# A two-layer encoder trunk on one core: order of the weight loads, arithmetic on GpSimd, and the output projections

## The chip, the cores and the metric

The kernel runs on one core of a Trainium2 chip. A core has TensorE (PE, matrix products; its weight loads are shown as PEld), VectorE (DVE), ScalarE (ACT), GpSimd (POOL) and SyncE (SP), which issues most of the transfers from HBM. The metric is the time of one execution in device microseconds, the median of three runs.

## What is computed

One sequence of 256 tokens with 1024 features passes two layers. Each layer is a token mixer and a mixture of experts (MoE), and each of the four sub-layers is normalized and scaled, shifted and gated by vectors that come from a conditioning vector c (adaLN). In short:

```python
for i in range(2):
    mod = silu(c) @ ada_w[i] + ada_b[i]                 # 6 x 1024
    sh1, sc1, g1, sh2, sc2, g2 = split(mod, 6)
    h = rms_norm(x, norm_mix_g[i]) * (1 + sc1) + sh1
    y = mla_mixer(h) if i == 0 else hyena_mixer(h)      # both end in a product with a 1024 x 1024 matrix
    x = x + g1 * y
    h = rms_norm(x, norm_ffn_g[i]) * (1 + sc2) + sh2
    x = x + g2 * hier_moe(h)                            # best of 4 groups, best 2 of its 4 experts
```

The attention (MLA) has 8 heads with low-rank q and kv. Hyena gates two long convolutions, done by Fourier transforms, whose filters come from a small network. Each of the 16 experts is a SwiGLU of 1024 to 256 to 1024. All is in 32-bit floats, so the large products run as sums of parts: a value is split into Hi (rounded) and Lo (the rest).

## The kernel before

The program runs the sub-layers one after another: attention (up to 183 us), router and MoE of layer 0 (to 361 us), Hyena (to 522 us), router and MoE of layer 1. Beside them two kinds of background work are spread into PE's gaps: the adaLN products for later sub-layers and the Hyena filters (`filt_unit`, eight units, three of them beside attention). Each engine runs its own list of instructions in order; a scheduler sets these lists when the program is built, by its own model of times, except where the code fixes the order.

Weights come through `Stream`, a ring of ten slots of 1 MB ("wt", 128 x 2048). A fixed list `order` says which block comes next; SP issues the next load as soon as a slot is free, one after the other. `st.done` gives a slot back, `st.temp` takes one for a temporary, `st.hold` keeps some free for temporaries. `moe_order` lists, for each pair of experts, four gate/up blocks (gu) and then the two down blocks (dn). The kernel computes gate and up of a pair in one step (`gate_up`) and its down product one step later (`down`). The list of attention is: five adas blocks, the four blocks of wo, the other nineteen adas blocks, and then the experts of layer 0.

An adas block is 1/8 of one of the adaLN products. `wide` (from L356) works it off as the string `WIDE` says: "p" is four matmuls of PE with the block (L389); "s" scales the block on ACT; "d" multiplies and adds on DVE (L370); "a" scales on ACT (L372) and adds on POOL (L373). "s", "d" and "a" gather several blocks into one, which then takes one product on PE. `PLAN` says how many blocks are handed out at each head of attention.

Other arithmetic on POOL before: two additions (L591) and a subtraction (L613) in each filter unit; in `split`, three of four Lo pieces of a wo block (L673; the Hi pieces are on ACT, L671); in `finish`, which adds the gated projection to x, the first half of each 128 tokens (L654; the second half on DVE, L656); in the router (`moe`), the quarters of xL, the low part of the normalized x that the experts' gather uses (L1198 and L1199, the last quarter on DVE, L1251); in `down` of layer 1, yL (L1422; in layer 0 on DVE).

Attention: `attend` takes the softmax (pr, L918 on ACT and L922 on DVE), transposes pr on PE (pT, L926), multiplies with v (oT, L931) and copies oT from PSUM on DVE (L932). The output projection comes behind the heads: for each of four wo blocks the parts oH (ACT) and oL (DVE, L956) of two heads are made, and 24 matmuls add to the four accumulators y_ps (L964). Hyena's projection has the same form, with accumulators psu (first tokens) and pse (second) and the line L1136.

The router goes from x to lg (logits), through short DVE operations L1215 to L1233 to sel (the chosen experts), to ct and rk on PE (L1239 to L1243), to the one-hot matrix OH on DVE (L1159), and to the gather xt_ps on PE (L1299, products of OH with xH and with xL), which the first gu_ps (L1388) follows. The lines L1210 start the accumulators acc with x.

## Time and profile before

| quantity | value |
|---|---|
| runs | 675.14, 676.16, 677.0 us |
| median | 676.16 us |
| profiled execution | 676.02 us |
| its span from first to last instruction | 674.2 us |
| mean granted clock of PE | 0.965 of full |

A profile belongs to one execution. The page gives, for each engine, how long it was busy. The table of stretches gives that for parts of the span, with the clock that PE was granted there (1.00 is full speed, 0.5 half). The list of waits says what ended PE's idle time: the engine, tile and line on the right of the arrow had to finish first. The views of single lines give what one instruction took.

### The profile page before, as it was taken

To read this page: it belongs to the slowest core of one execution; us is meant where nothing else is said; L and a number is where in the kernel's file an instruction comes from. 1 tells how busy PE (TensorE), PEld (TensorE's weight loads), DVE (VectorE), ACT (ScalarE), POOL (GpSimd) and SP (SyncE) were. 2 spreads that over 40 slices of the span, in tenths; PEclk is the share of its full clock that TensorE was granted. 3 is DMA by queue.
4 is the path that set the end of the run, shared out by engine and by line. 5 is a ranking of instruction groups with operands and counts; after the bars stand their busy time and mean duration, and the time that the engine had idled before them with its cause. 6 is when DMAs were issued, how large, how long until landed. Compare 5 with 4: busy or idle time off the path is not lost. (4 is left out here: it accounts for less than half of the span.)

```text
span 674.2 us, 8473 instructions
## 1 busy us (share of the span) xinstructions
PE 610.8 (91%) x3073; PEld 354.6 (53%) x3073; DVE 382.1 (57%) x826; ACT 234.8 (35%) x461; POOL 100.3 (15%) x130
## 2 busy tenths in 40 slices
PE   2998978979869899999996999999998799999996
PEld 0544435666646445445442888757776444344442
DVE  4527598898585354444567467578783832222222
ACT  2523556466243212212145554424613421111112
POOL 0001013348540000001000000000000400203023
PEclk9997998889988999989997999999999799999999
DMA  8997795664823879797987455694059368999801
GB/s 323 421 388 298 279 400 193 250 225 182 329 108 132 331 294 395 301 385 313 385 332 268 155 199 210 265 383 179 1 236 369 143 219 355 421 380 398 350 1 62
DMA packets 26819, 183.02 MB, mean 271 GB/s; under 512 B 3089, under 2 KB 3474, under 8 KB 5522
## 3 DMA queue, kind: packets, MB, share of 16 engines
q1 hardware_dynamic: 25920, 180.31, 68.2%
q10 hardware_dynamic: 850, 2.10, 0.9%
q8 instruction: 26, 0.43, 0.3%
q14 instruction: 23, 0.19, 0.1%
HBM read 181.35 MB, written 1.05 MB: 271 GB/s over the span
## 5 line engine op out<-in xcount | busy, mean ns | idle before, releaser
L1388 PE MATMUL gu_ps<-wt,XT 128*64 128x512 f32 x464 | 116.2, 604 | 7.3 <-DVEq L1452 4.2
L1388 PEld LDWEIGHTS gu_ps<-wt,XT 128*64 128x64 f32 x464 | 35.9, 138 | 69.9 <-issue 60.1
L1418 DVE TENSOR_TENSOR yg<-dn_ps,g1row 128x512 f32<-128x512 f32 x32 | 22.1, 691 | 83.5 <-PE dn_ps L1415 82.7
L1420 ACT CAST yH<-yg 128x512 fp32r<-128x512 f32 x32 | 19.8, 618 | 111.5 <-DVE yg L1418 110.4
L1415 PE MATMUL dn_ps<-wt,aT 128*64 128x512 f32 x208 | 53.6, 597 | 0.0
L1040 PE MATMUL psu<-hT,wt 128*128 128x256 f32 x192 | 44.9, 380 | 0.0
L1040 PEld LDWEIGHTS psu<-hT,wt 128*128 128x128 f32 x192 | 35.7, 190 | 9.3 <-issue 4.3
L1040 PE MATMUL psu<-zH,wt 128*128 128x256 f32 x192 | 37.9, 291 | 0.0
L1308 DVE TENSOR_SCALAR XT<-xt_ps,modA,modT 128x256 f32<-128x256 f32 x32 | 17.4, 542 | 35.5 <-ACT XT L1306 35.3
L1422 POOL TENSOR_TENSOR yL<-yg,yH 128x512 fp32r<-128x512 f32 x16 | 20.5, 1280 | 111.3 <-ACT yH L1420 110.8
L671 ACT CAST wt<-wt 128x512 fp32r<-128x512 f32 x56 | 30.8, 616 | 11.5 <-PE psu L1136 5.7
L673 DVE TENSOR_TENSOR wt<-wt 128x512 fp32r<-128x512 f32 x44 | 29.5, 709 | 6.8 <-POOL wt L673 2.4
L389 PE MATMUL ada_ps<-wt,csil 128*32 128x512 f32 x224 | 32.7, 616 | 0.1
L1306 ACT ACTIVATE XT<-xt_ps,modT,modA 128x256 f32<-128x256 f32 x32 | 17.9, 563 | 42.6 <-PE xt_ps L1299 42.5
L1040 PEld LDWEIGHTS psu<-zH,wt 128*128 128x128 f32 x192 | 30.1, 189 | 3.3 <-ACT up L1045 0.8
L1415 PEld LDWEIGHTS dn_ps<-wt,aT 128*64 128x64 f32 x208 | 16.3, 136 | 27.2 <-issue 25.9
L1299 PE MATMUL xt_ps<-OH,xH 128*128 128x256 f32 x128 | 28.7, 305 | 0.0
L1040 PE MATMUL psu<-zL,wt 128*128 128x256 f32 x96 | 27.7, 288 | 0.0
L1299 PEld LDWEIGHTS xt_ps<-OH,xH 128*128 128x128 f32 x128 | 21.2, 197 | 10.9 <-issue 4.2
L1299 PE MATMUL xt_ps<-OH,xL 128*128 128x256 f32 x128 | 26.4, 288 | 0.0
L1045 ACT ACTIVATE up<-psu,vec 128x256 f32<-128x256 f32 x24 | 11.4, 476 | 37.1 <-PE psu L1040 30.5
L1043 POOL MEMSET up<- 128x1 f32 x24 | 2.4, 100 | 141.9 <-DVE uc L1049 110.0
(367 smaller groups left out, 1227.0 us busy)
## 6 DMA issues: line engine op xcount, KB each, us to landing
wt<-in_gu SPq DMA_DIRECT2D x58, 1024.0 KB, 7.0
wt<-in_adas SPq DMA_DIRECT2D x40, 1024.0 KB, 5.7
wt<-in_dn SPq DMA_DIRECT2D x26, 1024.0 KB, 8.5
wt<-in_win SPq DMA_DIRECT2D x12, 1024.0 KB, 6.6
wt<-in_ada SPq DMA_DIRECT2D x8, 1024.0 KB, 17.3
wx<-in_dn SPq DMA_DIRECT2D x6, 1024.0 KB, 6.6
wx<-in_gu SPq DMA_DIRECT2D x6, 1024.0 KB, 8.0
wt<-in_wo SPq DMA_DIRECT2D x4, 1024.0 KB, 7.0
```

The source lines that it names most:

```text
L389: nc.tensor.matmul(q[g * 32:(g + 1) * 32, :], w.to_broadcast([P, 32]), W[:, g * 512:(g + 1) * 512], start=first, stop=(k == 7))
L671: nc.scalar.copy(Hi[:, sl], W[:, sl])
L673: eng.tensor_tensor(out=Lo[:, sl], in0=W[:, sl], in1=Hi[:, sl].bitcast(F32), op=ALU.subtract)
L1040: nc.tensor.matmul(q[:, :S], w[:, k, mm * P:(mm + 1) * P], h[:, k, :], start=(k == 0 and w is terms[0][0] and h is terms[0][1]), stop=(k = ...
L1299: nc.tensor.matmul(q[:, kk * 256:(kk + 1) * 256], src[:, t, k * P:(k + 1) * P], OH[:, t, :], start=(i == 0), stop=(i == 3))
L1306: eva = nc.scalar.activation(XT[:, k % 4, :], qv, AF.Identity, scale=a[:, k:k + 1], bias=b[:, k:k + 1])
L1308: evac[0] = nc.vector.tensor_scalar(XT[:, k % 4, :], qv, a[:, k:k + 1], b[:, k:k + 1], op0=ALU.mult, op1=ALU.add)
L1388: nc.tensor.matmul(q[i * 64:(i + 1) * 64, :], XT[h][:, k % 4, c0:c0 + CAP], GU[i][:, k % 4, :], start=(k == 0), stop=(k == 7))
L1415: nc.tensor.matmul(q[i * 64:(i + 1) * 64, :], aT[:, j, i * 64:(i + 1) * 64], DN[i][:, j, n * 512:(n + 1) * 512], start=(j == 0), stop=(j = ...
L1418: nc.vector.tensor_tensor(yg, q, grow[1][:, n * 512:(n + 1) * 512], op=ALU.mult)
L1420: nc.scalar.copy(yH, yg)
L1422: (nc.gpsimd if l else nc.vector).tensor_tensor(out=yL, in0=yg, in1=yH.bitcast(F32), op=ALU.subtract)
```

## The change

It has seven pieces.

1. Loads: wo comes behind all 24 adas blocks, and the dn blocks of a pair come behind the gu blocks of the next pair.
2. `WIDE`: mode "a" is gone. The second and third of its strings, which attention works off, are now "psddpppp" and "ppppsddd". With one product for each gathered sum, PE has 19 products in attention where it had 14; DVE has five blocks ("d") instead of seven, POOL none instead of three.
3. `filt_unit`, `finish`, `split`, the router's xL and yL of layer 1: what POOL did is done by DVE. In the router all four quarters of xL are one operation each, put behind the one-hot.
4. oH and oL are made at the end of each head, straight from PSUM, in two slots of the ring (`st.hold = 2` keeps them free); the copy of oT is gone.
5. A common `out_proj` for both projections: the first two blocks as before; then both last blocks for the first 128 tokens, and after that for the second. The slots of the last two blocks' parts come free at its end.
6. wo's first two blocks are split as before, beside the last heads.
7. In MoE of layer 0, the four slots for Hyena's first splits are held back from step 7 on instead of step 6.

```diff
-WIDE = ("pppppppp", "psdadadp", "ppsdaddd", "pppppppp", "pppppppp")
+WIDE = ("pppppppp", "psddpppp", "ppppsddd", "pppppppp", "pppppppp")
...
             for h in range(2):
                 for e in (2 * pr, 2 * pr + 1):
                     push("gu", l, e, h)
-            for e in (2 * pr, 2 * pr + 1):
-                push("dn", l, e)
+
+            for e in (2 * pr - 2, 2 * pr - 1):
+                if pr:
+                    push("dn", l, e)
+        for e in (14, 15):
+            push("dn", l, e)
...
-    for i, job in enumerate(seq):
-        if i == WO_AFTER:
-            push("wo")
+    for job in seq:
         push("adas", *job)
+    push("wo")
...
-            nc.gpsimd.tensor_tensor(out=a[:, 0, :], in0=a[:, 0, :], in1=a[:, 1, :], op=ALU.add)
+            nc.vector.tensor_tensor(a[:, 0, :], a[:, 0, :], a[:, 1, :], op=ALU.add)
...
-        nc.gpsimd.tensor_tensor(out=hh[1], in0=hh[0], in1=hh[1], op=ALU.subtract)
+        nc.vector.tensor_tensor(hh[1], hh[0], hh[1], op=ALU.subtract)
...
-                if n == 0:
-                    nc.gpsimd.tensor_tensor(out=x[:, t, sl], in0=x[:, t, sl], in1=tmp, op=ALU.add)
-                else:
-                    nc.vector.tensor_tensor(x[:, t, sl], x[:, t, sl], tmp, op=ALU.add)
+                nc.vector.tensor_tensor(x[:, t, sl], x[:, t, sl], tmp, op=ALU.add)
...
-            eng = nc.vector if alone or i == 3 else nc.gpsimd
-            eng.tensor_tensor(out=Lo[:, sl], in0=W[:, sl], in1=Hi[:, sl].bitcast(F32), op=ALU.subtract)
+            nc.vector.tensor_tensor(Lo[:, sl], W[:, sl], Hi[:, sl].bitcast(F32), op=ALU.subtract)
...
+    def out_proj(yq, zH, zL, cols, wo, name):
+        def part(j, t):
+            WH, WL = (w.rearrange("p (k n) -> p k n", k=2) for w in wo[j])
+            for kk in range(2):
+                k = 2 * j + kk
+                for z, W, f, l in ((zH, WH, 1, 0), (zL, WH, 0, 0), (zH, WL, 0, 1)):
+                    for n in range(2):
+                        nc.tensor.matmul(yq[t, n], z[:, k, cols(t)], W[:, kk, n * 512:(n + 1) * 512],
+                                         start=(k == 0 and f == 1), stop=(k == 7 and l == 1))
+
+        for j in range(2):
+            for t in range(2):
+                part(j, t)
+            st.give(2)
+            wo[j + 2] = split(name, j + 2)
+        for t in range(2):
+            for j in (2, 3):
+                part(j, t)
+        st.give(4)
...
+            st.hold = 2
...
-            oT = qT
+            oH, oL = (st.temp().rearrange("p (h s) -> p h s", h=H) for _ in range(2))
...
-                nc.vector.tensor_copy(oT[:, h, :], q[:, :S])
+                nc.scalar.copy(oH[:, h, :], q[:, :S])
+                nc.vector.tensor_tensor(oL[:, h, :], q[:, :S], oH[:, h, :].bitcast(F32), op=ALU.subtract)
...
-                            nc.gpsimd.tensor_scalar(xl, x[:, t, sl], r[:, t:t + 1], 0.0, op0=ALU.mult, op1=ALU.add)
-                        nc.gpsimd.tensor_tensor(xL[:, t, sl], xl, xH[:, t, sl].bitcast(F32), op=ALU.subtract)
...
-                nc.vector.scalar_tensor_tensor(out=xL[:, 1, 512:], in0=x[:, 1, 512:], scalar=r[:, 1:2], in1=xH[:, 1, 512:].bitcast(F32),
-                                               op0=ALU.mult, op1=ALU.subtract)
+                for n in range(2):
+                    sl = slice(n * 512, (n + 1) * 512)
+                    for t in range(2):
+                        nc.vector.scalar_tensor_tensor(out=xL[:, t, sl], in0=x[:, t, sl], scalar=r[:, t:t + 1], in1=xH[:, t, sl].bitcast(F32),
+                                                       op0=ALU.mult, op1=ALU.subtract)
...
-                        (nc.gpsimd if l else nc.vector).tensor_tensor(out=yL, in0=yg, in1=yH.bitcast(F32), op=ALU.subtract)
+                        nc.vector.tensor_tensor(out=yL, in0=yg, in1=yH.bitcast(F32), op=ALU.subtract)
...
-                    if step == 6 and l == 0:
+                    if step == 7 and l == 0:
```

Three places show what the change does to the engines' lists. The first is SP's list of loads from attention to the first router (adas and wo belong to attention, gu and dn to the first MoE). Before:

```order
L143 DMA wt<-in_wukv 128x2048
L143 DMA wt<-in_adas 128x2048 x5
L143 DMA wt<-in_wo 128x2048 x4
L143 DMA wt<-in_adas 128x2048 x19
L143 DMA wt<-in_gu 128x2048 x4
L143 DMA wt<-in_dn 128x2048 x2
L143 DMA wt<-in_gu 128x2048 x4
```

After:

```order
L142 DMA wt<-in_wukv 128x2048
L142 DMA wt<-in_adas 128x2048 x24
L142 DMA wt<-in_wo 128x2048 x4
L142 DMA wt<-in_gu 128x2048 x8
L142 DMA wt<-in_dn 128x2048 x2
```

The wo loads moved behind nineteen adas loads, and two dn loads behind the second four gu loads.

The second place is PE's list at the last heads of attention: pT_ps are the transposes of pr and oT_ps the products with v, four and two for a head; y_ps are the output projection. Before:

```order
L640 MATMUL lb_ps<-vec,modT_137 128x20 x8
L598 MATMUL fn_ps<-fgs,cst 32x128 x2
L931 MATMUL oT_ps<-pT,vv 128x256 x2
L598 MATMUL fn_ps<-fab,cst 32x128 x2
L926 MATMUL pT_ps<-cst,pr 128x128 x4
L389 MATMUL ada_ps<-wt,csil 32x512 x8
L931 MATMUL oT_ps<-pT,vv 128x256 x2
L964 MATMUL y_ps<-wt,oH 128x512
L964 MATMUL y_ps<-wt,oL 128x512
L964 MATMUL y_ps<-wt,oH 128x512
L964 MATMUL y_ps<-wt,oL 128x512
L964 MATMUL y_ps<-wt,oH 128x512 x2
```

After:

```order
L943 MATMUL pT_ps<-cst,pr 128x128 x4
L597 MATMUL fn_ps<-fab,cst 32x128 x2
L388 MATMUL ada_ps<-wt,csil 32x512 x16
L948 MATMUL oT_ps<-pT,vv 128x256 x2
L680 MATMUL y_ps<-wt 128x512 x4
L943 MATMUL pT_ps<-cst,pr 128x128 x4
L680 MATMUL y_ps<-wt 128x512 x6
L948 MATMUL oT_ps<-pT,vv 128x256 x2
L680 MATMUL y_ps<-wt 128x512 x20
L943 MATMUL pT_ps<-cst,pr 128x128 x4
L680 MATMUL y_ps<-wt 128x512 x6
L388 MATMUL ada_ps<-wt,cst 32x512 x3
```

Before, y_ps follows the last oT_ps; after, 36 y_ps matmuls stand ahead of the last heads' transposes or between them. On ACT the casts of wo (the Hi pieces) stand between the softmax operations of the last four heads, where before they followed all of them.

The third place is the end of Hyena's output projection on PE, psu for the first tokens and pse for the second. Before:

```order
L1136 MATMUL psu<-wt,zL 128x512 x2
L1136 MATMUL psu<-wt,zH 128x512 x4
L1136 MATMUL pse<-wt,zL 128x512 x2
L1136 MATMUL pse<-wt,zH 128x512 x2
L1136 MATMUL psu<-wt,zL 128x512 x2
L1136 MATMUL psu<-wt,zH 128x512 x2
L1136 MATMUL pse<-wt,zH 128x512 x2
L1136 MATMUL pse<-wt,zL 128x512 x2
L1136 MATMUL pse<-wt,zH 128x512 x2
```

After:

```order
L680 MATMUL psu<-wt,zL 128x512 x2
L680 MATMUL psu<-wt,zH 128x512 x4
L680 MATMUL pse<-wt,zL 128x512 x2
L680 MATMUL pse<-wt,zH 128x512 x2
L680 MATMUL psu<-wt,zL 128x512 x2
L680 MATMUL psu<-wt,zH 128x512 x2
L680 MATMUL pse<-wt,zH 128x512 x2
L680 MATMUL pse<-wt,zL 128x512 x2
L680 MATMUL pse<-wt,zH 128x512 x2
```

Nothing moved here: but for the line number the rows are the same, and those ahead of them too.

## Rows read from the trace of the kernel before

**Rows 1.** The page: each engine's busy us, share of the span, number of instructions.

```profile
PE 610.8 (91%) x3073; PEld 354.6 (53%) x3073; DVE 382.1 (57%) x826; ACT 234.8 (35%) x461; POOL 100.3 (15%) x130
```

**Rows 2.** Table of stretches: from:to, length, busy us (instructions) by engine, PEclk, DMA share, GB/s.

```profile
62.00:183.00 121.00, 108.37 (x536) 67.97 (x535) 96.70 (x194) 62.76 (x122) 46.01 (x28) 0.96 0.67 254
183.00:207.00 24.00, 16.90 (x103) 12.39 (x101) 19.46 (x49) 10.19 (x23) 8.45 (x9) 0.79 0.29 119
222.20:361.00 138.80, 134.12 (x668) 64.73 (x668) 66.20 (x125) 36.61 (x70) 9.28 (x16) 0.99 0.88 342
522.60:540.70 18.10, 13.47 (x82) 8.46 (x82) 14.68 (x38) 7.95 (x17) 7.11 (x7) 0.81 0.34 131
552.30:669.40 117.10, 116.13 (x540) 50.20 (x540) 30.13 (x67) 19.54 (x36) 20.48 (x16) 1.00 0.71 287
```

**Rows 3.** PE's waits, whole span: us in total, times, longest.

```profile
PE f_ps L514 <- DMA spec<-in_ab: 6.2, 1, 6.2
...
PE ct_ps L1239 <- DVE sel L1233: 4.4, 2, 3.0
...
PE xT_ps L1176 <- POOL x L654: 1.8, 2, 1.3
...
PE acc L1434 <- POOL yL L1422: 0.7, 2, 0.4
```

**Rows 4.** PE's waits from 62 to 183 us, attention.

```profile
PE pT_ps L926 <- DVE pr L922: 2.7, 1, 2.7
PE sc_ps L901 <- ACT kT L813: 1.6, 1, 1.6
PE ada_ps L389 <- DVE wt L370: 1.5, 1, 1.5
...
PE fh_ps L584 <- DVE den L920: 1.1, 1, 1.1
...
PE pT_ps L926 <- ACT pr L918: 0.8, 1, 0.8
```

**Rows 5.** View of the wo loads: the issues (duration, first to last start), and landing.

```profile
L143 SPq DMA_DIRECT2D wt<-in_wo x4: 327/328/328, 51.7 to 74.1; - x4
...
DMA to landing us min/median/max: 4.7/7.0/10.3
```

**Rows 6.** Views of single lines: ns min/median/max, first to last start us, forms.

```profile
L673 DVE TENSOR_TENSOR wt<-wt x44: 677/682/1781, 158.2 to 502.5; 128x512 fp32r<-128x512 f32 x44
L673 POOL TENSOR_TENSOR wt<-wt x12: 1337/1614/3155, 154.8 to 174.0; 128x512 fp32r<-128x512 f32 x12
...
L370 DVE SCALAR_TENSOR_TENSOR wt<-wt,csil x7: 2331/2339/2343, 103.2 to 154.5; 128x2048 f32<-128x2048 f32 x7
...
L373 POOL TENSOR_TENSOR wt<-wt x3: 4513/4518/4522, 107.8 to 139.1; 128x2048 f32<-128x2048 f32 x3
...
L922 DVE TENSOR_SCALAR pr<-pr,den x16: 333/344/3276, 115.1 to 151.0; 128x256 f32<-128x256 f32 x16
...
L1251 DVE SCALAR_TENSOR_TENSOR xL<-x,rq_y,xH x2: 742/744/746, 202.9 to 538.5; 128x512 fp32r<-128x512 f32 x2
...
L1422 DVE TENSOR_TENSOR yL<-yg,yH x16: 665/691/1805, 247.8 to 356.1; 128x512 fp32r<-128x512 f32 x16
L1422 POOL TENSOR_TENSOR yL<-yg,yH x16: 1269/1279/1298, 574.8 to 667.3; 128x512 fp32r<-128x512 f32 x16
```

**Rows 7.** PE's groups by shape, 62 to 183 us: busy us, mean ns | idle before.

```profile
L389 PE MATMUL ada_ps<-wt,csil 128*32 128x512 f32 x96 | 12.8, 599 | 0.0
```

**Rows 8.** DVE's groups by shape, 62 to 183 us.

```profile
L922 DVE TENSOR_SCALAR pr<-pr,den 128x256 f32<-128x256 f32 x16 | 8.8, 592 | 0.1
```

**Rows 9.** Timeline from 139 us: start us, us, engine, line, operation.

```profile
140.42 3.23 DVE L451 SCALAR_TENSOR_TENSOR modA<-modT,vec 128x8 f32<-128x8 f32 x1
```

**Rows 10.** Timeline of the first router.

```profile
197.69 1.27 DVE L1226 TENSOR_TENSOR gt<-gt,eq 128x160 f32<-128x160 f32 x1
```

**Rows 11.** Timeline of the second router.

```profile
530.93 4.69 PE L1210 MATMUL acc<-x,cst 128*128 128x512 f32 x6
```

60 lines of the change are left out of this document (9 added, 51 removed).

## The prediction

> **What bounds the kernel now.** I read the share of each engine first, then a table of stretches, then the list of what PE waits for, and last single lines and the timeline at the places those point to. The engine row [rows 1] says that PE is busy for 610.8 of 674.2 us, DVE for 382.1 and POOL for 100.3. So PE sets the time, and what can be won without taking work from PE is its 63.4 us of idle time and the time that it runs below full clock. The table of stretches [rows 2] says where that is. The two MoE layers are dense: 134.12 of 138.8 us and 116.13 of 117.1 us, at a granted clock of 0.99 and 1.00. The attention stretch from 62 to 183 us holds 108.37 of 121 us, so 12.6 us idle, at 0.96. The first router's stretch (183 to 207) holds 16.9 of 24 at 0.79, and the second's (522.6 to 540.7) 13.47 of 18.1 at 0.81.
>
> Now the waits of PE. Over the whole span [rows 3], apart from the first inputs, no weight block stands in the list as something that PE waits for: no expert block, no adas block, no wo block. What stands there is DVE and POOL work: 4.4 us for the routers' sel (3.0 of it in the first), 1.8 us for x of L654, 0.7 us for yL; and in attention [rows 4] 2.7 us for one pr, 1.6 for kT, 1.5 for an L370. So a better order of loads has nothing to take from PE before, and what I price is the move of arithmetic off POOL.
>
> **The change part by part.**
>
> *Order of loads.* The rows of SP show dn behind the next pair's gu, and wo behind all 24 adas blocks. With no weight wait on PE, the gain is 0. The loss is bounded by wo: a wo block lands within 10.3 us of its issue, 7.0 in the median, and all four were issued by 74.1 us [rows 5]; the first is split at about 155 us, where POOL's Lo pieces start [rows 6]. Now each wo block needs a slot that a consumed adas block gives back, so about the 14th to 18th of 24. These are consumed in the middle of attention, some 20 to 30 us ahead of the use, so I take 0 and keep +7.0 as the upper end. In MoE0, two temps more (oH, oL) and the four of the last wo pairs stay in the ring until the out-projection ends; but the DMA share from 183 to 207 us is 0.29 [rows 2], so eight late slots of 1 MB (8.4 MB, some 25 us at the MoE0 stretch's own 342 GB/s) have room there and in the 15 us behind. 0, with +2 as the upper end.
>
> *Wider adaLN row on PE.* Five blocks go from DVE and POOL to PE. One block is eight of the records of L389: 96 of them took 12.8 us [rows 7], so 8 x 12.8 / 96 = 1.07 us a block and 5 x 1.07 = +5.3 us of PE work, which is the largest loss in the change. PE in attention is then 108.4 + 5.3 = 113.7 us, and the stretch can't be shorter than that, apart from what the clock gives back. Against it: two L370 of 2.34 us leave DVE (-4.7), three L373 of 4.52 us leave POOL [rows 6], and their three scales leave ACT.
>
> *POOL's arithmetic to DVE in attention.* A Lo piece took 1.61 us on POOL in the median and 0.68 on DVE [rows 6]; twelve move, so 12 x 0.68 = 8.2 us of DVE. Three filter units add 3 x 1.5 = 4.5 us: two adds of half a Lo piece's columns, by my estimate 0.4 each, and a subtraction of its size. Eight copies of oT, of that half size too, go: -3.2. What DVE gets back is the stretching of its own work beside POOL. L922 has a median of 0.344 us [rows 6], and its mean is 0.592 [rows 8]: 16 x 0.25 = 4.0 us. One L451, an operation on 8 columns, took 3.23 us [rows 9], 2.9 more than an L922 of 256 columns. So DVE goes from 96.7 [rows 2] to at most 96.7 - 4.7 - 4.0 - 2.9 + 8.2 + 4.5 - 3.2 = 94.6 of 121 us: it doesn't become fuller, and its longest stall goes. That stall is the L451 just named: it lies beside the POOL L373 that began at 139.1 us [rows 6], pr comes behind it on DVE, and PE's transposes wait 2.7 us for pr [rows 4].
>
> The Trainium skill, page "SBUF — State Buffer", section "Who interferes with whom", says that DVE and GpSimd share a pair of ports, that an operation of two SBUF inputs contends with a GpSimd one that reads SBUF, and that one in a two-port mode blocks fully. This trace agrees for L922 (0.344 against a longest of 3.276). By the rows the sum has the 6.9 us of L922 and L451 back; by the rule every such operation beside POOL gets its time back, the other lines too, DVE ends below 94.6 us, and attention goes towards its lower bound below. No row tells how much that is, so I leave it out of the sum.
>
> What comes of it for PE: of 12.6 us idle in attention, five waits [rows 4] stand behind a step that goes or was stretched: pr 2.7, kT 1.6 (an adaLN scale stood ahead of it on ACT), L370 1.5, den 1.1 and pr again 0.8, 7.7 in all. They go, and I leave the other 4.9, since the softmax chain stays. PE at half clock after such gaps gives back some 1.5 of at most 0.04 x 121 = 4.8 us [rows 2]. Sum: +5.3 - 7.7 - 1.5 = **-3.9**; bounds +5.3 (+12 with late wo) and 5.3 - 12.6 - 4.8 = -12.1.
>
> *Output projection.* In attention the rows of PE show y_ps matmuls between the last heads, so it begins before the last oT. PE's work is the same (its filling of gaps is already in the -7.7). For "half of the tokens first" the rows show less: in Hyena's projection they are the same before and after, to the last matmul, psu ending six matmuls ahead of pse. This part is worth 0 there, bounds -1 and +1.
>
> *First router.* On the way to sel the DVE operations stretch beside POOL's xL: one of 160 columns took 1.27 us [rows 10], nearly four times an L922 of 256 columns. PE's ct waits 3.0 us for sel there [rows 3], and no more than that can be won; without the stretching I count 2.7 of it. On the other side, three more xL on DVE at 0.742 [rows 6] come behind the one-hot, 2.2 us, where PE's gather of OH and xL follows; the gather's first matmuls need only xH and the first quarters, so I count half, +1.1. The x sums of L654 go to DVE: one addition of a Lo piece's size in place of a POOL one, but in a row with the other, 0. I take **-1.6**, bounds -5 and +2.
>
> *Second router.* Here ct waits 1.4 us for sel (4.4 less 3.0 [rows 3]), since PE's own six acc matmuls, 4.69 us long [rows 11], end only at 535.62; 1.4 is the most to win. PE waits 1.8 us for POOL's x here [rows 3]; but gy, gy, x, x now stand in a row on DVE, so the sums end as late as before, and that wait changes its owner. Less some 0.5 for xL: **-0.9**, bounds -2 and +2.
>
> *yL in MoE1.* 0.691 on DVE for 1.279 on POOL [rows 6]; PE's wait of 0.7 us for it [rows 3] goes: **-0.7**, bounds -1 and 0. DVE is busy for 30 of 117 us there [rows 2], so it has room. MoE0's filter adds are under its dense PE: 0, bounds -3 and +2.
>
> Sum: -3.9 - 1.6 - 0.9 - 0.7 = -7.1. The profiled execution took 676.0 us (span 674.2 and 1.8 around it), and the median of the runs is 676.16, 0.1 more. 676.0 - 7.1 = 668.9, so **669 us**.
>
> **The rivals.** A run can tell a difference of about 0.3% (2 us) from none: 674.1 to 678.2 is "same".
>
> *Slower: PE pays for the adaLN blocks and wo comes late.* The place is the stretch from 130 to 183 us. ACT takes its work in order; its casts of wo now stand ahead of the last heads' softmax, so if wo has not landed, the softmax waits behind it, and PE behind that. It decides when the 14th adas block is consumed later than some 7 to 10 us ahead of the first cast. Then the 5.3 us of PE work fall on a stretch that keeps its idle time, with 3 to 7 us more: 676 + 5.3 + 3 - 3.2 (the routers and yL) = 681, up to 684. For it: the 5.3 us are certain, the covered idle time is not. Against: PE's list shows no load that was ever late, and the 10 slots run ahead.
>
> *No difference.* DVE takes the place of POOL as what is late: in attention it stays at three quarters of the time, and a serial chain softmax - oL - Lo gives each gap a new owner; then attention gives 0 to -1, the first router half of its 1.6, the rest 1: 674 to 676. For it: DVE is busy for 96.7 of 121 us of attention [rows 2]. Against: part of that is stretching.
>
> *A much larger gain.* All gaps and the half clock of attention and the first router go: -12.1 - 5 - 2 = 657. For it: the low clock follows the gaps, so fewer gaps give twice. Against: 5.3 us more PE work and an unchanged softmax chain.
>
> *The change does not do what it says.* The rows already show that for the Hyena projection; it is 0 in every case above.
>
> **How the numbers follow.** Forecast, 662 to 673 around 669: 0.50. Larger gain, 655 to 661: 0.15. No difference, 674 to 678: 0.16. Slower, 679 to 684: 0.19. So faster 0.65, same 0.16, slower 0.19. The range leaves out the longest of the slower cases (0.14) and the lowest of the large gains (0.05): 657 to 680.
>
> **What would show it.** Attention's stretch up to the last y_ps should be 4 us shorter, with PE busy for about 113 us, no DVE operation of 8 to 256 columns over 1 us, and no wait for pr of 2.7 us. Between the last y_ps and the first gu 2 us less. MoE0, Hyena and its projection as long as before. I am wrong if casts of wo or any matmul wait for a DMA there, if PE's idle time in attention stays at 12 us, or if the xL quarters are what the gather waits for by more than 2 us.

## The result, and the profile after

The changed kernel took 682.56 us in the median of eight runs (681.49 to 683.88), the kernel before 676.80 us in the same measurement. The ratio is 1.0082, with a 95% interval from 1.0065 to 1.0100: the change makes the kernel slower by 0.8%. The forecast was 669 us with a range from 657 to 680, so the measured time lies outside it and on the other side of no change. The profiled execution took 682.93 us, its span is 681.1 us. One execution each of e5, e7, e11 and of the kernel before (in the measurement of e9 to e12) fell in a slower state, and no ratio below counts it.

The engines' row of the page, which answers to [rows 1]:

```profile
PE 623.3 (92%) x3113; PEld 353.8 (52%) x3113; DVE 379.3 (56%) x878; ACT 226.8 (33%) x456; POOL 6.1 (1%) x61
```

POOL is nearly empty, as the change says. DVE took over 52 more instructions and is yet busy for 2.8 us less; PE has 40 matmul records more and is busy for 12.5 us more. To see where, I cut both spans at the same events: first q and kv product, last y_ps, first gu and last acc of layer 0, first and last matmul of Hyena, first gu and last acc of layer 1. The columns are those of [rows 2]. Kernel before:

```profile
61.27:182.47 121.20, 108.57 (x536) 67.87 (x535) 96.95 (x196) 62.76 (x122) 45.48 (x28) 0.96 0.67 254
182.47:207.28 24.81, 17.71 (x107) 13.07 (x105) 19.95 (x49) 10.47 (x23) 8.98 (x9) 0.79 0.30 125
207.28:358.81 151.53, 144.18 (x718) 70.43 (x721) 74.45 (x149) 38.68 (x72) 10.71 (x14) 0.99 0.85 328
366.45:522.55 156.10, 153.92 (x824) 116.08 (x824) 105.16 (x195) 64.45 (x124) 3.73 (x45) 0.99 0.58 227
522.55:540.66 18.11, 13.43 (x82) 8.41 (x81) 14.69 (x38) 7.95 (x17) 7.16 (x7) 0.81 0.34 132
540.66:669.42 128.76, 126.42 (x593) 54.84 (x592) 35.81 (x91) 23.12 (x42) 20.48 (x16) 1.00 0.70 279
```

Changed kernel:

```profile
60.94:185.43 124.49, 116.54 (x583) 70.22 (x582) 85.26 (x213) 58.20 (x121) 0.90 (x3) 0.95 0.63 241
185.43:205.33 19.90, 14.87 (x104) 10.01 (x102) 19.13 (x55) 8.61 (x19) 0.30 (x1) 0.91 0.60 234
205.33:364.27 158.94, 149.35 (x716) 70.07 (x719) 75.06 (x158) 38.27 (x72) 0.90 (x3) 0.97 0.79 308
371.68:527.35 155.67, 153.49 (x824) 116.68 (x824) 104.91 (x195) 63.91 (x123) 2.91 (x44) 0.99 0.59 229
527.35:545.40 18.05, 13.78 (x82) 8.64 (x81) 13.75 (x45) 7.32 (x16) 0.00 (x0) 0.81 0.34 129
545.40:676.41 131.01, 127.31 (x593) 54.95 (x592) 45.44 (x106) 22.76 (x42) 0.00 (x0) 1.00 0.69 276
```

The second column is the length. Attention grew by 3.3 us, the first router fell by 4.9, MoE of layer 0 grew by 7.4, Hyena and the second router stayed within 0.5, and MoE of layer 1 grew by 2.25. So the router gave more than forecast, and the largest loss lies in a stretch where the forecast had 0, and where PE has two records fewer than before. Its granted clock fell from 0.99 to 0.97 and its idle time rose from 7.35 to 9.6 us.

**What went as forecast: the stretching is gone.** The views of single lines, and DVE's groups in attention (L939 is the old L922, L1204 the old L1226, L1403 yL, L668 the Lo pieces):

```profile
L939 DVE TENSOR_SCALAR pr<-pr,den 128x256 f32<-128x256 f32 x16 | 4.9, 341 | 0.1
...
L1204 DVE TENSOR_TENSOR gt<-gt,eq x2: 326/326/326, 197.1 to 537.2; 128x160 f32<-128x160 f32 x2
...
L1403 DVE TENSOR_TENSOR yL<-yg,yH x32: 683/692/693, 251.3 to 674.9; 128x512 fp32r<-128x512 f32 x32
...
L668 DVE TENSOR_TENSOR wt<-wt x56: 680/685/693, 150.3 to 507.3; 128x512 fp32r<-128x512 f32 x56
```

pr took 592 ns in the mean beside POOL's arithmetic [rows 8] and takes 341 without it; the comparison of 160 columns took 1.27 us [rows 10] and takes 0.326; the longest Lo piece on DVE took 1.781 us [rows 6], now 0.693. DVE in attention went from 96.95 to 85.26 us, below the 94.6 that I gave as the most. By the Trainium skill, page "SBUF — State Buffer", section "Who interferes with whom", a DVE operation contends with GpSimd when it has two SBUF inputs and the GpSimd operation reads SBUF, or when it runs in a two-port mode. The rows agree with it for the comparison and the Lo pieces, which have two such inputs; whether pr, which has one, runs in such a mode no row shows. In the first router PE's wait for sel fell from 3.0 us [rows 3] to 0.6.

**What did not: PE in attention.** PE's groups of adas products, which answer to [rows 7], and a piece of the timeline:

```profile
L388 PE MATMUL ada_ps<-wt,csil 128*32 128x512 f32 x136 | 22.1, 671 | 0.0
L388 PE MATMUL ada_ps<-wt,cst 128*32 128x512 f32 x16 | 4.0, 832 | 1.5 <-DVE wt L372 1.5
```

```profile
106.74 0.46 PE L597 MATMUL fn_ps<-fgs,cst 128*32 128x128 f32 x2
108.73 1.93 PE L388 MATMUL ada_ps<-wt,cst 128*32 128x512 f32 x8 [1.53 <-DVE wt L372]
110.43 1.88 PE L388 MATMUL ada_ps<-wt,csil 128*32 128x512 f32 x8
```

There are 152 records instead of 112, the 40 that were forecast. But a block of eight takes 1.9 us here against 1.07 before: the granted clock is at its lower level (0.5, 1.2 GHz) from 105.3 to 112.1 us, after PE had waited 1.9, 0.9 and 2.6 us at matmuls of a filter unit, and again from 142.9 to 149.7 us. Of the 152 records 16 start in each of these two stretches; of the 112 before, none started at the low clock. The waits of PE in attention, which answer to [rows 4]:

```profile
PE fn_ps L597 <- DVE fgs L590: 2.6, 1, 2.6
PE dl_ps L566 <- DVE rq_i L459: 1.9, 1, 1.9
PE ada_ps L388 <- DVE wt L372: 1.5, 1, 1.5
PE fh_ps L583 <- DVE fh L586: 0.9, 1, 0.9
PE oT_ps L948 <- ACT pT L945: 0.7, 1, 0.7
```

The waits for pr and kT are gone, as forecast; the one for an adas block on DVE stays. At matmuls of the filter units PE waits 5.4 us (2.6, 1.9 and 0.9), about as much as before (5.0 in five waits), and the longest is new: fgs L590 is one of the additions that the change moved, and on DVE it stands behind an L372 of 2.35 us. e2 below has the additions on POOL and does not have this wait. Idle time fell from 12.6 to 7.95 us. No wait ended on a weight load here.

**MoE of layer 0.** PE at the branch of the first expert step, kernel before and then changed kernel, and last one later step of the changed kernel with DVE:

```profile
222.14 7.09 PE L1388 MATMUL gu_ps<-wt,XT 128*64 128x512 f32 x32 [2.79 <-DVEq L1452]
```

```profile
220.70 0.41 PE L597 MATMUL fn_ps<-fgs,cst 128*32 128x128 f32 x4 [2.06 <-DVE fh L586]
222.14 9.19 PE L1369 MATMUL gu_ps<-wt,XT 128*64 128x512 f32 x26 [1.02 <-PEq L1433]
231.26 0.41 PE L597 MATMUL fn_ps<-fab,cst 128*32 128x128 f32 x4
231.60 1.93 PE L1369 MATMUL gu_ps<-wt,XT 128*64 128x512 f32 x6
```

```profile
314.23 0.44 PE L1387 MATMUL at_ps<-cst,aa 128*128 128x128 f32 x2
314.37 1.28 DVE L608 TENSOR_TENSOR fh<-fh,fi_ps 128x512 f32<-128x512 f32 x2 [0.19 <-PE fi_ps L606]
315.57 0.54 DVE L1289 TENSOR_SCALAR XT<-xt_ps,modA,modT 128x256 f32<-128x256 f32 x1
316.02 0.47 DVE L1379 SCALAR_TENSOR_TENSOR aa<-sg,ws,gu_ps 128x256 f32<-128x256 f32 x1
...
316.55 0.79 PE L1369 MATMUL gu_ps<-wt,XT 128*64 128x512 f32 x2 [1.88 <-DVE aa L1379]
```

At the branch PE waits twice, 2.06 us for a filter operation (fn waits for fh on DVE) and 1.02 us for the branch itself. The kernel before waited 2.79 us there, for DVE's queue, so the wait grew by 0.3 us only, and the difference lies in what follows. The clock is at its lower level from 221.4 to 228.2 us, so the next 26 gu matmuls take 9.19 us; before, 32 of them took 7.09. And fn products now stand between the gu matmuls. By their starts in the trace, gu and dn matmuls run two by two, a pair every 0.43 us at the full clock, and one without a partner takes the 0.43 us alone: the 26 and the six behind fn are 14 pairs and four single ones, 18 such places, where the 32 before are 16 pairs. In the later step DVE has two filter operations (L608) and an XT in its list ahead of aa, and PE's gu waits 1.88 us. Neither place has anything to do with a load.

Three terms make up the 7.4 us of the stretch, by my estimate: idle time grew by 2.2 us; the clock is low for 10.2 us of it (3.4 before), which at half the clock costs 3.4 us more; and 24 of the 384 gu and dn matmuls have no partner (16 before), four places of 0.43 us more, 1.7.

### The profile page after: what moved, and what is told of

Read it like the earlier page. It is cut to its first block, busy times and chain, and to the rows that moved or that the text cites. A ratio compares the mean times of both kernels' runs of the same rounds, so it can differ in the third digit from the quotient of the medians.

```text
span 681.1 us, 8491 instructions
## 1 busy us (share of the span) xinstructions
PE 623.3 (92%) x3113; PEld 353.8 (52%) x3113; DVE 379.3 (56%) x878; ACT 226.8 (33%) x456; POOL 6.1 (1%) x61
## 5 line engine op out<-in xcount | busy, mean ns | idle before, releaser
L1369 PE MATMUL gu_ps<-wt,XT 128*64 128x512 f32 x448 | 118.4, 621 | 6.2 <-DVE aa L1379 3.8
L1399 DVE TENSOR_TENSOR yg<-dn_ps,g1row 128x512 f32<-128x512 f32 x32 | 22.1, 689 | 74.0 <-PE dn_ps L1396 73.3
L1396 PE MATMUL dn_ps<-wt,aT 128*64 128x512 f32 x224 | 56.5, 597 | 0.0
L388 PE MATMUL ada_ps<-wt,csil 128*32 128x512 f32 x264 | 41.1, 651 | 3.0 <-DMA wt<-in_adas 3.0
L668 DVE TENSOR_TENSOR wt<-wt 128x512 fp32r<-128x512 f32 x56 | 36.1, 686 | 5.8 <-ACT wt L667 4.2
L1403 DVE TENSOR_TENSOR yL<-yg,yH 128x512 fp32r<-128x512 f32 x32 | 22.1, 690 | 15.9 <-ACT yH L1401 15.8
L1280 PEld LDWEIGHTS xt_ps<-OH,xH 128*128 128x128 f32 x128 | 20.7, 194 | 12.3 <-issue 4.3
L680 PE MATMUL y_ps<-wt 128*128 128x512 f32 x96 | 24.8, 404 | 0.0
```

What stands on the lines that cost most here:

```text
L388: nc.tensor.matmul(q[g * 32:(g + 1) * 32, :], w.to_broadcast([P, 32]), W[:, g * 512:(g + 1) * 512], start=first, stop=(k == 7))
L668: nc.vector.tensor_tensor(Lo[:, sl], W[:, sl], Hi[:, sl].bitcast(F32), op=ALU.subtract)
L680: nc.tensor.matmul(yq[t, n], z[:, k, cols(t)], W[:, kk, n * 512:(n + 1) * 512], start=(k == 0 and f == 1), stop=(k == 7 and l == 1))
L1280: nc.tensor.matmul(q[:, kk * 256:(kk + 1) * 256], src[:, t, k * P:(k + 1) * P], OH[:, t, :], start=(i == 0), stop=(i == 3))
L1369: nc.tensor.matmul(q[i * 64:(i + 1) * 64, :], XT[h][:, k % 4, c0:c0 + CAP], GU[i][:, k % 4, :], start=(k == 0), stop=(k == 7))
L1396: nc.tensor.matmul(q[i * 64:(i + 1) * 64, :], aT[:, j, i * 64:(i + 1) * 64], DN[i][:, j, n * 512:(n + 1) * 512], start=(j == 0), stop=(j = ...
```

## The experiments

Sixteen kernels, each compared with runs of the kernel before on the same chip. Lengths of stretches are those of one profiled execution, cut at the events above. In the tables "attn", "rout", "MoE 0" and "MoE 1" are the lengths in us. A ratio compares a kernel with the kernel before in the same measurement, where the latter's median was between 675.2 and 677.1 us; so from row to row compare the ratios rather than the medians.

| run | attn | rout | MoE 0 | MoE 1 | median | ratio (95%) |
|---|---|---|---|---|---|---|
| before | 121.2 | 24.8 | 151.5 | 128.8 | 676.8 | |
| changed | 124.5 | 19.9 | 158.9 | 131.0 | 682.56 | 1.0082 (1.0065 to 1.0100) |
| e1 | 123.8 | 23.2 | 149.9 | 131.0 | 676.52 | 1.0006 (0.9976 to 1.0037) |
| e2 | 121.6 | 23.4 | 149.2 | 131.0 | 674.94 | 0.9975 (0.9946 to 1.0004) |
| e3 | 124.5 | 20.7 | 157.2 | 129.3 | 681.16 | 1.0058 (1.0032 to 1.0085) |
| e4 | 124.5 | 20.7 | 158.4 | 128.3 | 679.43 | 1.0037 (1.0009 to 1.0065) |
| e5 | 123.8 | 22.0 | 150.0 | 128.8 | 675.24 | 0.9954 (0.9930 to 0.9979) |
| e6 | 124.0 | 25.3 | 150.0 | 129.8 | 681.35 | 1.0065 (1.0033 to 1.0097) |
| e7 | 123.0 | 21.2 | 154.6 | 128.8 | 676.95 | 0.9993 (0.9962 to 1.0025) |
| e8 | 121.7 | 23.4 | 152.3 | 128.3 | 672.59 | 0.9923 (0.9894 to 0.9952) |
| e9 | 123.9 | 22.1 | 158.7 | 131.0 | 682.30 | 1.0060 (1.0031 to 1.0088) |
| e10 | 122.8 | 21.1 | 150.8 | 128.3 | 673.24 | 0.9933 (0.9904 to 0.9961) |
| e11 | 130.4 | 25.5 | 144.4 | 128.8 | 676.88 | 0.9998 (0.9963 to 1.0032) |
| e12 | 119.9 | 20.9 | 155.5 | 135.1 | 680.89 | 1.0061 (1.0035 to 1.0086) |
| e13 | 123.4 | 22.5 | 150.0 | 131.0 | 675.45 | 0.9996 (0.9978 to 1.0013) |
| e14 | 124.4 | 21.1 | 151.5 | 128.3 | 672.80 | 0.9951 (0.9932 to 0.9970) |
| e15 | 124.7 | 20.7 | 155.7 | 131.0 | 681.00 | 1.0079 (1.0051 to 1.0106) |
| e16 | 125.3 | 21.4 | 156.4 | 128.3 | 679.74 | 1.0033 (1.0011 to 1.0055) |

### One part of the change undone: e1 to e4

e1, WIDE back:

```diff
-WIDE = ("pppppppp", "psddpppp", "ppppsddd", "pppppppp", "pppppppp")
+WIDE = ("pppppppp", "psdadadp", "ppsdaddd", "pppppppp", "pppppppp")
...
+                nc.scalar.activation(W, W, AF.Copy, scale=w)
+                nc.gpsimd.tensor_tensor(out=acc, in0=acc, in1=W, op=ALU.add)
```

> The changed kernel with the old strings of WIDE: three adas blocks go back to a scale on ACT and an addition on POOL, two to DVE, and PE has 14 products in attention again where it has 19. All else is as in the changed kernel (median 682.6 us, ratio 1.008). Theory (the five products of PE are the loss of attention: their 10.5 us, half of it at half clock, outweigh 4.7 us less idle time): the adas records of PE fall from 152 to 112 and from 24.7 to some 14 to 17 us, the last y_ps comes 3 to 6 us earlier than the 185.4 us of the changed kernel, and the time is 676 to 679 us. Rival (attention lost by its new order, the wo splits and out-projection between the heads, and PE's products only fill gaps): the last y_ps stays within 1.5 us of 185.4, and the time within 681 to 684 us.

The last y_ps stayed at 185.28 us: for attention the rival holds. Yet the time fell by 6 us, to where the theory had it, and by nothing that the theory named: MoE of layer 0, which does not use the changed strings, fell from 158.9 to 149.9 us.

e2, filter additions back on POOL:

```diff
-            nc.vector.tensor_tensor(a[:, 0, :], a[:, 0, :], a[:, 1, :], op=ALU.add)
+            nc.gpsimd.tensor_tensor(out=a[:, 0, :], in0=a[:, 0, :], in1=a[:, 1, :], op=ALU.add)
...
-        nc.vector.tensor_tensor(hh[1], hh[0], hh[1], op=ALU.subtract)
+        nc.gpsimd.tensor_tensor(out=hh[1], in0=hh[0], in1=hh[1], op=ALU.subtract)
```

> The changed kernel with the additions and subtractions of the eight filter units back on POOL. Theory (MoE of layer 0 lost 7.4 us because filter work on DVE now stands in front of the branch of the first expert step, PE waits 2.1 us for it, and the low clock that follows stretches the next 9 us): the stretch from the first gu to the last acc of layer 0 falls from 158.9 us to 152 to 155 us, and the time to 676 to 679 us. Rival (the loss comes from elsewhere, such as the order of the down blocks or where the stretches of low clock fall): the stretch stays at 157 to 160 us, and the time at 681 to 684 us.

Both fell, and further than the theory had: MoE of layer 0 to 149.2 us, the time to 674.94. But e1 gives the same stretch with the additions on DVE. So "filter additions on DVE" can't be the cause in MoE of layer 0 as it stands; what the two have in common had to be looked for in PE's list (e13).

In attention it is otherwise. The stretch of e2:

```profile
61.55:183.13 121.58, 116.39 (x583) 69.52 (x582) 83.66 (x202) 57.58 (x121) 12.37 (x12) 0.94 0.60 230
```

PE is as busy as in the changed kernel (116.39 and 116.54 us), but idle for 5.2 us instead of 7.95, and the stretch is 2.9 us shorter. The wait of 2.6 us for fgs is gone. So in attention the additions on DVE are most of the 3.3 us; e8, with the same edit, has 121.7 us and 5.1 us idle.

e3, the down blocks' order back, and e4, yL back on POOL:

```diff
-            for e in (2 * pr - 2, 2 * pr - 1):
-                if pr:
-                    push("dn", l, e)
-        for e in (14, 15):
-            push("dn", l, e)
+            for e in (2 * pr, 2 * pr + 1):
+                push("dn", l, e)
...
-                    if step == 7 and l == 0:
+                    if step == 6 and l == 0:
```

> The changed kernel with the old order of the experts' loads: the two down blocks of a pair right behind its gate and up blocks, and four slots held back from step 6 on. wo stays behind the adas blocks. Theory (no PE wait on an expert block in either kernel, so this part is worth nothing): 681 to 684 us, and MoE of layer 0 within 1.5 us of 158.9 us. Rival (the order of the loads is what cost MoE of layer 0 its 7.4 us): MoE of layer 0 at 152 to 154 us and the time at 675 to 678 us.

681.16 us and MoE of layer 0 at 157.2, 1.7 us less than in the changed kernel: the order of the experts' loads is not the cause of the 7.4. MoE of layer 1 fell by 1.7 us too, to 129.3, which the theory did not have; see e4.

```diff
-                        nc.vector.tensor_tensor(out=yL, in0=yg, in1=yH.bitcast(F32), op=ALU.subtract)
+                        (nc.gpsimd if l else nc.vector).tensor_tensor(out=yL, in0=yg, in1=yH.bitcast(F32), op=ALU.subtract)
```

> The changed kernel with yL of the second layer back on POOL. Theory (yL on DVE stands in front of DVE's other work of the same step, OHT, ws and aa, for which PE then waits, and that made MoE of layer 1 longer by 2.25 us): its stretch from the first gu to the last acc falls from 131.0 us to 128.5 to 129.5 us, and the time by 1.5 to 2.5 us, to 680 to 681.5 us. Rival (the 2.25 us come from the end of the list alone, where the last two pairs' down products were reordered, whoever makes yL): the stretch stays at 130.5 to 131.5 us and the time at 682 to 683 us.

MoE of layer 1 fell from 131.0 to 128.3 us, a little more than the theory had; the time to 679.43. The waits of PE in that stretch, changed kernel and then e4:

```profile
PE gu_ps L1369 <- DVEq L1433: 1.4, 1, 1.4
PE acc L1415 <- DVE yL L1403: 0.8, 1, 0.8
PE gu_ps L1369 <- DVE aa L1379: 0.7, 3, 0.2
PE at_ps L1387 <- DVE ws L1313: 0.6, 3, 0.2
```

```profile
PE gu_ps L1369 <- DVEq L1433: 1.4, 1, 1.4
PE acc L1415 <- POOL yL L1403: 0.4, 1, 0.4
```

yL itself is half as long on DVE, and PE waits longer for it (0.8 for 0.4): there it stands in a row with yg, OHT, ws and aa, and PE waits for these as well. On POOL it ran beside them. But yL's engine is not all of it: e3 has yL on DVE, waits 0.6 us for it, and is only 0.5 us longer than the kernel before in this stretch. What e3 and e4 share is the number of gu and dn matmuls without a partner, 12 as in the kernel before, where the changed kernel has 16 (0.9 us by my estimate). So the 2.25 us come from yL on DVE together with the new order of the down blocks; to undo either gives most of it back.

### One part alone on the kernel before: e5, e6, e7, e11, e12

e5, wo behind the adas blocks:

```diff
-    for i, job in enumerate(seq):
-        if i == WO_AFTER:
-            push("wo")
+    for job in seq:
         push("adas", *job)
+    push("wo")
```

> The kernel before (676.2 to 676.8 us) with one change: the wo blocks are loaded behind all 24 adas blocks. Theory (the order of loads is worth nothing either way, since no PE wait ended on a weight block): the last y_ps stays at 181 to 184 us and the time at 675 to 678 us. Rival (wo late, or the adas blocks early, is what made attention 3 us longer in the changed kernel): the last y_ps at 185 to 187 us, the time at 678.5 to 681 us.

The ratio is 0.9954: a little faster, where the theory had no difference (the median lies in its range). Attention grew by 2.6 us, with the last y_ps at 187.9, which was the rival's place but not its result. The router and MoE of layer 0 gave more than that back. PE waited for no load in these three stretches, so what moved can only be where the scheduler places the work; that is argued and not shown further.

e6 adds the new projections to e5 (the functions `out_proj` and `attend` of the change, POOL keeps its arithmetic).

> The kernel before with late wo and the new output projections (oH and oL made from PSUM at the end of each head, the first two wo blocks' products between the last heads, the last two for the first tokens first); the arithmetic that POOL has stays there, and so does WIDE. Theory (the new projection is what made attention longer: the last heads' softmax now has y_ps matmuls and wo casts in between, and its end is later than what the filled gaps give): the last y_ps at 184.5 to 187 us and the time at 678 to 681 us, with Hyena's projection as long as before. Rival (the projection fills gaps and gains, and attention's 3 us come from the filter work and the adaLN products ahead of it): the last y_ps at 178 to 182.5 us and the time at 671 to 676 us.

The median was 681.35 us over a wide spread (677.09 to 685.97), and the profiled execution is its lowest, with the last y_ps at 182.1 us and Hyena's projection as before. Its stretches can't explain the median, so this run is inconclusive; e9 asks the same from the other side.

e7, all of xL on DVE:

```diff
...
-                            nc.gpsimd.tensor_scalar(xl, x[:, t, sl], r[:, t:t + 1], 0.0, op0=ALU.mult, op1=ALU.add)
-                        nc.gpsimd.tensor_tensor(xL[:, t, sl], xl, xH[:, t, sl].bitcast(F32), op=ALU.subtract)
...
+                for n in range(2):
+                    sl = slice(n * 512, (n + 1) * 512)
+                    for t in range(2):
+                        nc.vector.scalar_tensor_tensor(out=xL[:, t, sl], in0=x[:, t, sl], scalar=r[:, t:t + 1], in1=xH[:, t, sl].bitcast(F32),
+                                                       op0=ALU.mult, op1=ALU.subtract)
```

> The kernel before with one change: in both routers all four quarters of xL are made on DVE behind the one-hot, none on POOL. Theory (the short DVE operations up to sel were stretched by POOL's xL): in the first router the seven operations from eq to sel take 2 to 3 us instead of 5.5, the first gu comes 1.5 to 3 us earlier than 207.3 us, in the second router nothing to 1 us is won, and the time is 673 to 675 us. Rival (three more operations of 0.74 us behind the one-hot give it all back): the first gu within 1 us of 207.3, the time 675.5 to 678 us.

The routers fell by 3.6 us (24.8 to 21.2) and 1.8 us (18.1 to 16.3), more than the theory had, and the time did not move (0.9993): MoE of layer 0 grew by 3.0 us and attention by 1.8. The first gu came at 207.3 us as before. So the rival's two numbers came, but not for its reason: the gain in the routers is real, and attention ahead of the first one and MoE of layer 0 behind it gave it back.

e11, the filter additions on DVE, the reverse of e2's edit on the kernel before:

> The kernel before with one change: the additions and the subtraction of the filter units are made on DVE. Theory (filter operations on DVE stand ahead of aa and of the branch, whatever the rest of the kernel does): MoE of layer 0 grows from 151.5 us to 155 us or more, and the time to 679 to 684 us. Rival (what costs in the changed kernel is the stage that the filter units have reached when the first expert step starts, which moving attention's work shifts; DVE's 1.5 us more for a unit do nothing by themselves): MoE of layer 0 at 149 to 153 us and the time at 674 to 678.5 us.

The rival holds in the time, 676.88 us. The stretches show why none of them may be read alone: attention grew by 9.2 us and MoE of layer 0 fell by 7.1 to 144.4, below the rival's range. PE has 11 records more in attention and 9 fewer in MoE of layer 0, and the clock's mean went from 0.96 to 0.91 in the one and from 0.99 to 1.00 in the other: filter work and low clock moved ahead.

e12, the new WIDE alone, the reverse of e1's edit on the kernel before:

> The kernel before with the new strings of WIDE alone: 19 products of PE in attention, five blocks on DVE, none on POOL. Theory (5.3 us more PE work and about as much idle time less, a wash, as undoing it on the changed kernel showed, where the last y_ps moved by 0.2 us): the time 674.5 to 678.5 us, PE's idle time in attention 12.6 us before and 6 to 9 us here. Rival (PE's 5.3 us come on top): 680 to 683 us.

The time was the rival's (680.89 us), the mechanism was not. Attention became shorter, 119.9 us, with PE's idle time down from 12.6 to 6.6 us. MoE of layer 0 grew by 3.9 us, and MoE of layer 1 by 6.3 us, where the kernel's text is that of before. The second of these is at the branch:

```profile
549.88 0.48 DVE L1398 SCALAR_TENSOR_TENSOR aa<-sg,ws,gu_ps 128x256 f32<-128x256 f32 x1
...
555.28 1.12 PE L1388 MATMUL gu_ps<-wt,XT 128*64 128x512 f32 x2 [6.12 <-DVEq L1452]
```

DVE's last operation ahead of the branch ends at 550.4 us, its queue goes on at 555.2, and PE waits 6.12 us where the kernel before waits 1.4. Less that, by one execution, the new WIDE is a wash, as e1 said.

### The stage of the filter work: e13 to e15

PE's lists show what e1 and e2 have in common. At the end of the list ahead of the branch, changed kernel (fh_ps and fn_ps are two stages of a filter unit, fn waits for DVE and ACT to work off fh):

```
L1308 MATMUL oht_ps<-tok,OH_1808 128x160 x2
L583 MATMUL fh_ps<-fwH,hs 128x256
L584 MATMUL fh_ps<-fwL,hs 128x256
L583 MATMUL fh_ps<-fwH,hs 128x256
L584 MATMUL fh_ps<-fwL,hs 128x256
L597 MATMUL fn_ps<-fgs,cst 32x128 x2
L1433 COMPARE_AND_BRANCH
```

In e1 and e2, and with one more entry in the scheduler's table of priorities (e13), fh stands one expert step earlier:

```
L1308 MATMUL oht_ps<-tok,OH_1808 128x160 x2
L597 MATMUL fn_ps<-fgs,cst 32x128 x2
L1369 MATMUL gu_ps<-wt,XT 64x512 x4
L1308 MATMUL oht_ps<-tok,OH_1808 128x160 x2
L597 MATMUL fn_ps<-fab,cst 32x128 x2
L1433 COMPARE_AND_BRANCH
```

The same difference runs on through the later steps. e3, e4 and e9, at 157 to 159 us, have the changed kernel's list; e2, e8 and e10, at 149 to 152, the other. e13 changes this and nothing else:

```diff
-FILT = {6: -400000, 7: 400000}
+FILT = {3: -400000, 6: -400000, 7: 400000}
```

> The changed kernel (682.6 us) with one number more in the table of the scheduler's priorities: filter unit 3 is put back, so that at the branch of the first expert step the filter work has reached another stage (the same list of PE from there on as in the kernels with the old WIDE, or with the filter additions on POOL). No operation changes its engine. Theory (MoE of layer 0 lost its time by the stage at which the filter work meets the expert steps, not by DVE's additions as such): its stretch from the first gu to the last acc falls from 158.9 us to 149 to 153 us, and the time to 674 to 679 us. Rival (DVE's filter additions are the loss, and in the runs with the additions on POOL they were what helped): the stretch stays at 156 to 160 us, and the time at 680 to 684 us.

675.45 us, and MoE of layer 0 at 149.98 us: the theory's numbers. All arithmetic is where the change put it. Its stretch, and PE at the branch:

```profile
205.44:355.42 149.98, 142.25 (x709) 68.01 (x712) 73.23 (x155) 37.87 (x71) 0.91 (x3) 0.99 0.85 327
```

```profile
220.37 8.78 PE L1369 MATMUL gu_ps<-wt,XT 128*64 128x512 f32 x32 [2.75 <-DVEq L1433]
```

Of the 9.0 us between the two kernels in this stretch, 1.9 are idle time (9.6 and 7.7 us). The clock is low for 10.2 us in the changed kernel, after the branch (221.4 to 228.2) and after the wait of 1.88 us (316.9 to 320.3), and for 3.4 in e13, after the branch; that makes 3.4 us, by my estimate. Matmuls without a partner, 24 and 16, make 1.7. The rest, some 2 us, is filter work that e13 does ahead of the first gu (709 records for 716; its router is 2.6 us longer). So the gain over both stretches is 6.4 us.

e14, the same with yL on POOL as in e4:

> The same, with yL of the second layer on POOL as well: two changes to the changed kernel. Theory (two losses in two stretches, which add up): 671 to 675 us, below the kernel before. Rival (the filter stage only moves the time to attention or to the router): 678 to 682 us.

672.80 us, ratio 0.9951: the two losses add up, and the kernel is faster than both.

e15, another entry (unit 5 instead of 3): the list up to the branch is the changed kernel's, behind it another one.

> The changed kernel with filter unit 5 put back instead of unit 3: PE's list is that of the changed kernel up to the branch of the first expert step, and another one behind it. Theory (both halves count: PE's wait and the low clock around the branch cost some 4 us, the filter operations of DVE ahead of aa in the later steps some 4 us): MoE of layer 0 at 153 to 156 us, the time at 677 to 681 us. Rival (all of it is the branch): the stretch at 157 to 160 us and the time at 681 to 684 us.

155.7 us and 681.0 us, at the theory's edge; but the ratio, 1.0079, is that of the changed kernel (1.0082), so in the time this entry gave nothing back, as the rival had it. The wait for fn (2.07 us) and for the branch (1.03) is there again, with no low clock behind it in this execution, and 32 gu matmuls in a row took 7.09 us as before. So the price of the place at the branch depends on where the clock falls, and how the loss divides between the branch and the later steps is not shown.

### Combinations: e8, e9, e10, e16

e8 is e2 and e4 together.

> The changed kernel with both the filter units' additions and the second layer's yL back on POOL, the two parts that cost something when they were undone one at a time. Theory (the two losses lie in different stretches and add up): 674.9 us of the kernel with the filter additions back, less the 2.7 us that yL was worth in MoE of layer 1, so 671 to 673.5 us, below both kernels. Rival (they share one cause, such as DVE's load, or where the low clock falls): 674 to 677 us.

672.59 us, ratio 0.9923, as the theory had it; with e10 and e14 the fastest.

e9 undoes the new projections in the changed kernel, e10 in e8.

> The changed kernel (682.6 us) with the old output projections of both layers; the rest, late wo and no arithmetic on POOL, as changed. Theory (the new projection costs what it cost on the kernel before with late wo, where the median went from 675.2 to 681.4 us): the time falls to 676 to 679 us, and the last y_ps comes earlier than 185.4 us. Rival (that cost came from mixing it with POOL's Lo pieces; without POOL the projection is neutral, and the changed kernel's loss is the filter work on DVE): 681 to 684 us.

> The kernel with the filter additions and the second layer's yL on POOL (672.6 us) with the old output projections as well. Theory (the projection's cost is independent of the filter work): 667 to 670.5 us. Rival (once POOL's work no longer stretches DVE there, the new projection is what fills attention's gaps, and undoing it loses): 673 to 677 us.

682.30 and 673.24 us: in both cases no difference beyond the interval. The new projections, half of the tokens first among them, are worth nothing here. That leaves e6's median without an explanation.

e16 takes the five products from PE in e14 and gives the blocks to DVE:

```diff
-WIDE = ("pppppppp", "psddpppp", "ppppsddd", "pppppppp", "pppppppp")
+WIDE = ("pppppppp", "psdddddp", "ppsddddd", "pppppppp", "pppppppp")
```

> The kernel with the filter stage moved and yL of the second layer on POOL (672.8 us) with the old count of products in WIDE, and no POOL: the strings psdddddp and ppsddddd, so 14 products of PE in attention instead of 19, and ten blocks on DVE instead of five. PE's list in MoE of layer 0 is the same. Theory (PE bounds attention; of the 5.3 us of products some 2 to 4 us are not covered by idle time, while DVE, at 85 us of 124 us, has room for 11.7 us more): PE's work in attention falls from 111.4 to some 106 us, its stretch to the last y_ps from 123.4 to 124.4 us to 119.5 to 122 us, and the time to 669 to 671.5 us. Rival (DVE gets late, and the softmax waits for it): PE's idle time rises from 8 to 12 us and more, the stretch stays at 123 to 126 us, and the time at 672 to 676 us.

The rival holds for attention, which was 125.3 us against 124.4: PE's work fell by 6.6 us and its idle time rose by 7.5, most of it in one wait:

```profile
PE fi_ps L606 <- DVE fwH L250: 7.7, 1, 7.7
PE fn_ps L597 <- DVE fgs L590: 2.6, 1, 2.6
```

So DVE has no room for these blocks where they fall, though it is busy for only 95.7 of 125.3 us, and PE's 5.3 us for them are covered. The time, 679.74 us, is above the rival's range too. In the profiled execution, the slowest of twelve (674.9 to 681.2), some 4 us are a late branch as in e12, here of layer 0 (PE waited 6.51 us, e13 2.75); whether it is in the other executions no trace shows.

## Why the prediction was wrong, point by point

- **MoE of layer 0: the step that failed.** I put the filter additions there "under its dense PE: 0, bounds -3 and +2". Measured +7.4. The step looked at how much work DVE would have, which was right (74.45 to 75.06 us), and not at where the filter work would stand in PE's and DVE's lists when the expert steps begin: 2.2 us more idle time, some 3.4 us of low clock and some 1.7 us of matmuls without a partner. I had the two lists at hand, and compared them in attention and in Hyena, not at the branch. e13 shows the cause: one entry in a table of priorities gives 7 us of the median back, 6 by the ratios.
- **Attention, -3.9 forecast, +3.3 measured.** The stretching went, more than forecast. Of the five waits of 7.7 us those for pr and kT went and the one for an adas block stayed; I put no new wait against them, and the moved addition made one of 2.6 us, so idle time fell by 4.7 us. e2 shows it: without that wait idle time falls by 7.4. The five products were sized at the full clock, 5.3 us; 32 of the 152 records ran at half of it in two places, and PE's busy time rose by 8.0 us. I had given the clock a gain of 1.5 us; it was low for 13.7 us instead of 10.2, a loss of some 1.7. These are the second and third terms that were mis-sized.
- **First router, -1.6 forecast, -4.9 measured.** Right in mechanism and too small: the wait for sel fell from 3.0 to 0.6 us, the clock rose from 0.79 to 0.91, and PE did not wait for xL here, where I had put 1.1 us. e7 shows it alone: -3.6 us. Part of the -4.9 is only moved, since the changed kernel does filter work in MoE of layer 0 that e13 does here: there the router gives -2.3.
- **Second router, -0.9 forecast, -0.1 measured.** The wait for sel went, and PE's ct came 2.3 us earlier, counted from the end of Hyena. The gather lost the same again: from ct to the first gu it took 5.9 us for 3.6, in which PE waits 0.5 us for xL and 0.7 for the mask m, which now stand in a row on DVE. I had 0.5 for that. The wait for x stayed (1.6 us for 1.8), as the text said.
- **yL, -0.7 forecast, +2.25 measured.** I compared the two durations of one operation. e4 shows that its row on DVE counts: PE waits for what stands behind it. e3 shows that the order of the down blocks has a part in it.
- **Order of loads: 0.** e3 agrees for the experts, but for the 1.7 us in each MoE stretch. (The text names six slots that come late and prices eight; the term is 0 with either.) No wo cast waited for a load. PE waits 3.0 us for an adas block, between MoE of layer 0 and Hyena, and not before the change; that stretch is no longer for it (7.41 us for 7.64), and e12, with the old order, has such a wait as well (3.5). And the rival of a late wo did not happen; its time, 681 to 684 us, came by another cause. For the kernel before alone, late wo gave -0.5% (e5), and not through a wait of PE for a load in attention, router or MoE.
- **Half of the tokens first: 0.** Hyena's stretch is 155.7 against 156.1 us, and e9 and e10 agree.

The terms measured sum to 3.3 - 4.9 + 7.4 - 0.1 + 2.25 = 8.0, and -1.1 from the start, Hyena and the stretch ahead of it: 6.9 us, the difference of the two spans.

## What to carry to other kernels

Where a scheduler orders the work, a change of engine is two changes: what the operation costs, which the trace tells, and where all lists then meet, which only the lists tell. Compare the lists at every hand-over, above all where background work stands ahead of a branch or of the operation that the matrix engine waits for. And an operation that is twice as fast on a busy engine can still be worse there than beside it: count its row, not its duration.

## What was not expected of the hardware

- The taken branch at the start of the expert steps cost DVE different times in kernels whose code there is the same. DVE's queue went on within 0.1 us after its last operation at 33 of the 36 branches of the eighteen traces, but 0.8 us later in e6, 4.8 us later in e12 and 3.8 us later in e16 (one of two branches each). No row shows what it waited for; it isn't settled.
- The clock is not the same in every execution of a kernel: its mean in the kernel before ranged from 0.961 to 0.974. The medians of the kernel before ranged from 675.2 to 677.1 us over six measurements, and single executions from 673.6 to 681.3. A difference of stretches of under 2 us in two profiles is therefore not evidence by itself; that of MoE of layer 0 between 149 to 152 us (e1, e2, e8, e10, e13, e14) and 157 to 159 us (the changed kernel, e3, e4, e9) is. e16 has the list of the first six and took 156.4 us, with the late branch.
